# Adding each expert's rows to the output in memory with an indirect DMA, in place of one-hot products on TensorE

## Chip, cores and metric

The kernel runs on one core of one Trainium2 chip, as one launch. The metric is device time in microseconds (us), the median of several runs. TensorE is called PE here, VectorE DVE, ScalarE ACT, GpSimd POOL and SyncE SP.

## What is computed

The reference is an encoder of two layers over 256 tokens of 1024 float32 values. Layer 0 mixes with long convolutions and has a dense feed-forward part; layer 1 mixes with attention and has a mixture of 8 experts, each token going to its best two. The change touches only the mixture:

```python
def moe_swiglu(h, router, wg, wu, wd):
    ...
    logits = jnp.dot(hf, router, preferred_element_type=jnp.float32)
    top_v, top_i = lax.top_k(logits, TOP_K)
    gates = jax.nn.softmax(top_v, axis=-1).reshape(A)
    ...
    def expert_block(args):
        xe, e = args
        return (jax.nn.silu(xe @ wg[e]) * (xe @ wu[e])) @ wd[e]

    yb = lax.map(expert_block, (xb, blk_expert)).reshape(P, D)
    out = jnp.zeros((T, D), jnp.float32).at[buf_tok].add(yb.astype(jnp.float32) * buf_gate[:, None])
```

The result is `x + moe_swiglu(...)`: each expert's rows are multiplied by the gates of their tokens and added to the tokens' rows. The hidden width is 2816.

## The kernel before

**Products in parts.** Every float32 operand is split into two float32r parts, high and low (`Pair`): ACT copies the high part, DVE subtracts it from the source for the low part (`split`), and PE makes three products (`mm3`). So each half unit of weights, 128x1024, costs one ACT cast, one DVE subtraction and six products of 128x512.

**The stream of weights.** An expert's weights are 33 units of 1 MB. `weights` loads them one after another on SP's DMA queue into slots of 8 KiB per partition, and splits them by halves. Up to `N_SPLIT = 4` split halves may stand ready ahead of their products. There are 8 x 33 = 264 such loads.

**The order of the program.** The program is recorded as a plain sequence. `Plan.order` then sorts it against a simple model of the engines, gives every tile its place, and emits one queue per engine; it is the same code for the whole program. Waits are added afterwards. On the chip each engine goes through its queue in order, so an instruction that waits holds up all that stand behind it on its engine.

**An expert.** The 256 tokens stand as two tiles of 128 (`a` = 0, 1). A place of an expert is one of 128 rows that it works on. `gather` makes one-hot matrices `oh[a]` (token by place) on DVE and multiplies the tokens with them, for two experts at a time. It also transposes the one-hot matrices on PE into `ohT` (place by token). `expert` then makes six blocks of gate and up columns, each followed by the rows of down of the block before it, which sum up in two banks `py[0]`, `py[1]` (the two halves of 512 columns). At the end each bank is split into two parts, multiplied back to the tokens with `ohT`, and added to `x` with the tokens' gates:

```python
        for c in range(2):
            y = self.pair(512)
            self.split(y, py[c])
            for a in range(2):
                ps = self.bank()
                nc.tensor.matmul(ps, lhsT=ohT[:, a], rhs=y.hi, start=True, stop=False)
                nc.tensor.matmul(ps, lhsT=ohT[:, a], rhs=y.lo, start=False, stop=True)
                xa = self.x[a][:, c * 512:(c + 1) * 512]
                nc.vector.scalar_tensor_tensor(xa, ps, gate(a), xa, op0=OP.mult, op1=OP.add)
                if last:
                    self.store((a, c))
```

The last expert stores the four quarters of `x` to the output. A second round follows under `tc.If(most > 128)`, for experts with more than 128 tokens; its code is in the program, but no load of it is in the trace.

Of the kernel before, what the change touches and what calls it, by code (L numbers as in the profile page):

```python
# [21 lines left out]
D = 1024  # L22
S = 256
# [8 lines left out]
# columns of the table of per-partition scalars  # L32
# [6 lines left out]
# columns of the table of constants  # L39
K_ID, K_FLIP, K_TRI, K_ONE, K_IOTA, K_I8, K_FOLD = 0, 128, 256, 384, 512, 640, 648  # L40
N_K = 656

# [53 lines left out]
class Mem:  # L96
    """A tile: kind 'sb' (n words in the slots), 'ty' (a few words), 'ps' (a bank), 'at' (fixed)."""
# [8 lines left out]
class Slot:  # L106
    """A slot from the time it is taken until all of it is free again: of one type."""
# [22 lines left out]
LOAD = 1.3  # L130


class Plan:
# [45 lines left out]
    def pin(self, v):  # L179
        """Keep a whole slot beyond the next flush."""  # L180
        assert v.t.size == SLOT
        v.t.pinned = True
        self.fixed.append(v.t)

# [47 lines left out]
    def fits(self, op):  # L232
        """Whether the tiles that op is the first to touch can have a place now."""
# [16 lines left out]
        # what more urgent tiles will take soon  # L250
# [22 lines left out]
        if op.kind == "split" and self.n_split >= N_SPLIT:  # L273
            # only if a product waits for nothing else
            if not any(self.ops[j].n_pred == 1 and self.ops[j].eng == "tensor" for j in op.succ):
                return False
        return sum(m.kind == "ps" for m in need) <= max(0, len(self.free_bank) - banks)

# [18 lines left out]
    def cost(self, eng, fn, a, kw, aps):  # L297
        """Microseconds on the engine."""
        n = max((self.width(x) for x in aps), default=1)
        if fn == "dma_start":  # L300
            ap = aps[0]
            return self.width(ap) * ap.ap[0][1] * 4 / 360e3
# [68 lines left out]
    def order(self):  # L371
        ops = self.ops
        following = 1e9
        for op in reversed(ops):
            late = op.base
            own = op.dur + (2.0 if op.fn == "dma_start" else 0.0)
# [4 lines left out]
            if op.kind == "dense":  # L381
                # products with the stream keep their order
                op.late = following = min(op.late, following - op.dur)
# [23 lines left out]
        while done < len(ops):  # L407
            self.stuck = not events
            if self.stuck:
                # nothing runs: the most urgent operation takes from the reserves  # L410
# [20 lines left out]
            for e in engines:  # L431
                if busy[e] > t or not avail[e]:
                    continue
                if e == "sync" and dma > t + BACKLOG:
                    # loads that become urgent meanwhile go first
# [16 lines left out]
                if e in ("vector", "scalar") and op.i != self.force and op.dur > 0.2:  # L452
                    # better to wait a moment for what is more urgent
# [14 lines left out]
                else:  # L468
                    end = busy[e] = t + op.dur
                    f = op.args[2] if op.fn == "activation" else None  # L470
# [23 lines left out]
    def backwards(self):  # L494
        """Latest starts that keep to one operation at a time on every engine: the schedule from the
        end, the latest by the first estimate first."""
# [46 lines left out]
    def profile(self):  # L543
        """Slots that tiles other than the stream's hold, by the time of the latest starts."""
# [15 lines left out]
    def flush(self):  # L560
        """Order and emit what was recorded."""
        out = self.order()
        real = lambda x: x.on(self.place(x.t)) if isinstance(x, View) else x
        with self.tc.manual_schedule():
            for op in out:
                getattr(getattr(self.nc, op.eng), op.fn)(*[real(x) for x in op.args],  # L566
                                                         **{k: real(x) for k, x in op.kw.items()})
# [3 lines left out]
class Pair:  # L571
    """The two exact float32r parts of a float32 tile."""
# [16 lines left out]
def _par(t):  # L589
    """Natural order of positions -> [.., parity, place]."""  # L590
# [3 lines left out]
class _Kernel:  # L594
# [8 lines left out]
    def pair(self, n):  # L603
        """Both parts of [128, n]."""
# [45 lines left out]
    def rsqrt(self, ss, n, width):  # L650
        """(ss / width + EPS) ** -0.5, with one Newton step."""
# [10 lines left out]
    def rms(self, src):  # L662
        """One over the root mean squares of src [128, D]."""
# [8 lines left out]
    def norm_T(self, src, dst):  # L672
        """Two tiles of tokens -> the transposes of the rows over their root mean squares."""
# [15 lines left out]
    def scaled(self, dst, col, natural=False):  # L689
        """The parts of the transposes times a gain."""  # L690
# [8 lines left out]
    def head_norms(self, ps, lo, hi, rms=None):  # L699
        """Two banks of 4 heads -> the heads lo..hi-1 over their rms, two tiles."""  # L700
# [20 lines left out]
    def heads_T(self, ps, dst, scale=None, rms=None):  # L721
        """Two banks of raw heads -> dst parts [128 d, 4, 2, 128 tok]."""
# [9 lines left out]
    def dense_block(self, lhs):  # L732
        """512 columns for both token tiles: two banks."""
# [9 lines left out]
    def softmax_rows(self, ps, groups, p):  # L743
        """[128, groups, width] -> p, normalised."""
# [16 lines left out]
    def tokens(self, src):  # L761
        """[256, D] in DRAM: tile a has the tokens 2 p + a."""
# [7 lines left out]
    def rows_of(self, ps, dst, rms):  # L770
        """Two banks of rows -> parts [128, 2, 512]."""
# [3 lines left out]
    def cross(self, qps, kT, v, gain, mixT):  # L775
        """Attention over the memory."""
# [22 lines left out]
    def out_proj(self, mixT, order):  # L799
        """x += both halves of the mix by the weights of the output."""  # L800
# [23 lines left out]
    def run(self):  # L824
# [3 lines left out]
        # w_out by (q, c) within a half: the halves of a unit are (c, q)  # L828
# [19 lines left out]
        self.fold = kt[:2 * NE, K_FOLD:K_FOLD + 8]  # L848
        self.mhalf = plan.at([128, 8], "mhalf")
        nc.gpsimd.memset(self.mhalf, -0.5)  # L850
        # the sine's table, before anything waits for it
# [15 lines left out]
    def taps(self):  # L867
        """The hidden layer that makes the filters, in two versions: forward + and - backward."""
# [18 lines left out]
        # the second layer twice, for the products with both directions at once  # L887
# [7 lines left out]
        # the backward filter has no place 0  # L895
# [21 lines left out]
                # |f| + |b| is the larger of |f + b| and |f - b|  # L917
# [10 lines left out]
            # one over the sums, by channel  # L928
# [72 lines left out]
    def channels_T(self, us):  # L1001
        """Their transposes: two banks [128 tokens, 512]."""
# [92 lines left out]
    def memory(self, l, keys):  # L1095
        """Keys (transposed) or values of the memory."""
# [498 lines left out]
```

## Time and profile before

| what | value |
|---|---|
| time, median of 3 runs | 1338.82 us (1338.54 to 1339.26) |
| span of the profiled execution | 1336.3 us, 2.5 us less than the median |
| PE busy | 1316.9 us, 99% of the span |
| DVE, ACT, POOL busy | 1111.6, 918.3, 25.9 us |
| moved by DMA | 368.12 MB, 275 GB/s over the span |

The span is from the first to the last instruction of one execution; what lies around it is in the time and not in the profile. Products are pipelined: a row's duration of a product reaches from its start to its modelled end, and is longer than the distance from its start to the next one's. All recorded instructions of the plan bear line 566, where they are emitted, so groups are told apart by tiles: `s` is a slot, `b` a bank, `tiny` a few words per partition, `x` the tokens, `kt` the constants, `out` the output.

### The profile page before, as it was taken

How to read it: one execution, taken by the hardware profiler on the slowest of the kernel's cores; microseconds unless marked ns; L12 is line 12 of the kernel's file. 1: busy time of each engine (PE TensorE's matmuls, PEld its weight loads, DVE VectorE, ACT ScalarE, POOL GpSimd, SP SyncE). 2: the span in 40 equal slices, each digit the busy share in tenths (PEclk: the TensorE clock that was granted, in tenths of full speed). 3: DMA queues.
4: the chain of work that ended last, by engine and by line, in shares of the span. 5: the costliest groups of instructions: out<-in, count | busy, mean ns of one | idle time of the engine just before them, and what ended most of it. 6: DMA issues, size and time to landing. Idle time of an engine off the chain costs nothing.

```text
span 1336.3 us, 17095 instructions
## 1 busy us (share of the span) xinstructions
PE 1316.9 (99%) x6320; PEld 1087.2 (81%) x6320; DVE 1111.6 (83%) x1440; ACT 918.3 (69%) x1196; POOL 25.9 (2%) x30
## 2 busy tenths in 40 slices
PE   6999999999999999999999999999999999999997
PEld 4798888888878888888888888888888888888875
DVE  7999775554578776899999998999999999988987
ACT  7455754444566665787777777777777777777774
POOL 0100000000001000000000000000000000000000
PEclk9999999999999999999999999999999999999999
DMA  9648534357446356199899888999889898899994
GB/s 354 241 153 294 211 126 157 125 189 271 145 138 210 122 194 253 64 348 354 346 356 356 333 332 346 344 346 339 348 334 364 320 344 345 344 346 357 344 368 161
DMA packets 56430, 368.12 MB, mean 275 GB/s; under 512 B 6303, under 2 KB 10483, under 8 KB 12692
## 3 DMA queue, kind: packets, MB, share of 16 engines
q1 hardware_dynamic: 56340, 366.97, 73.9%
q8 instruction: 51, 0.84, 0.2%
q14 instruction: 39, 0.32, 0.1%
HBM read 365.87 MB, written 1.07 MB: 275 GB/s over the span
## 4 chain that ended last, share of the span: by engine, by line
PE 96%; DVE 1%; ACT 1%; issue 0%; DMA 0%; SPq 0%; DVEq 0%; ACTq 0%
PE b L566 96%; ACT s L566 1%; DVE s L566 1%; DMA sm<-sm 0%; DVE x L566 0%; SPq L566 0%; DVE tiny L566 0%; DVE cg L566 0%; DVEq L566 0%; ACTq L566 0%
## 5 line engine op out<-in xcount | busy, mean ns | idle before, releaser
L566 PE MATMUL b<-s,s 128*128 128x512 f32 (+4 forms) x5708 | 1282.3, 382 | 5.0 <-ACT s L566 4.3
L566 PEld LDWEIGHTS b<-s,s 128*128 128x128 f32 (+2 forms) x5708 | 1012.8, 188 | 213.0 <-issue 7.2
L566 DVE TENSOR_TENSOR s<-s,s 128x1024 fp32r<-128x1024 f32 (+2 forms) x729 | 839.4, 1188 | 137.4 <-ACT s L566 132.4
L566 ACT CAST s<-s 128x1024 fp32r<-128x1024 f32 (+2 forms) x705 | 710.0, 1039 | 248.1 <-PE b L566 203.9
L566 DVE TENSOR_TENSOR s<-b,s 128x512 f32<-128x512 f32 (+5 forms) x222 | 133.3, 614 | 32.2 <-ACT s L566 29.6
L566 ACT CAST s<-b 128x512 fp32r<-128x512 f32 (+3 forms) x142 | 69.8, 507 | 69.5 <-PE b L566 62.4
L566 PE MATMUL b<-kt,s 128*128 128x128 f32 (+1 forms) x496 | 88.9, 274 | 1.1 <-DVE s L566 0.9
L566 PEld LDWEIGHTS b<-kt,s 128*128 128x128 f32 x496 | 66.7, 146 | 19.4 <-ACT s L566 2.2
L566 ACT ACTIVATE s<-b 128x512 f32<-128x512 f32 (+3 forms) x81 | 42.9, 539 | 19.7 <-PE b L566 19.7
L566 DVE SCALAR_TENSOR_TENSOR s<-b,sm,s 128x256 fp32r<-128x256 f32 (+1 forms) x88 | 37.9, 477 | 8.1 <-ACT s L566 7.4
L566 ACT ACTIVATE s<-b,sm 128x256 fp32r<-128x256 f32 (+1 forms) x84 | 35.1, 484 | 12.2 <-PE b L566 7.9
L566 ACT ACTIVATE s<-b,tiny 128x256 f32<-128x256 f32 (+2 forms) x42 | 23.6, 580 | 15.4 <-PE b L566 13.5
L566 POOL TENSOR_TENSOR tiny<-tiny,mhalf 128x1 f32<-128x1 f32 (+4 forms) x23 | 25.4, 1106 | 340.8 <-DVE tiny L566 340.8
L566 PE MATMUL b<-s 128*128 128x512 f32 (+3 forms) x70 | 20.4, 380 | 5.8 <-DMA s<-fw 5.6
L566 DVE SCALAR_TENSOR_TENSOR x<-b,gate,x 128x512 f32<-128x512 f32 x32 | 22.5, 746 | 1.2 <-PE b L566 0.9
L566 ACT ACTIVATE s<-x 128x512 f32<-128x512 f32 x16 | 10.0, 630 | 14.3 <-PE b L566 5.2
L566 DVE TENSOR_TENSOR tiny<-tiny 128x1 f32<-128x1 f32 (+4 forms) x81 | 11.9, 154 | 8.3 <-ACT s L566 6.5
L566 PEld LDWEIGHTS b<-s 128*128 128x128 f32 (+1 forms) x70 | 12.2, 189 | 8.0 <-DMA s<-fw 5.6
L566 DVE TENSOR_REDUCE tiny<-b 128x2 f32<-128x512 f32 (+2 forms) x17 | 11.1, 657 | 8.3 <-PE b L566 8.3
L566 DVE TENSOR_REDUCE tiny<-s 128x4 f32<-128x512 f32 (+3 forms) x26 | 13.9, 556 | 3.6 <-ACT s L566 3.5
L566 ACT COPY s<-b 128x512 f32<-128x512 f32 x11 | 6.4, 588 | 14.6 <-PE b L566 13.8
L566 DVE TENSOR_TENSOR x<-b,x 128x512 f32<-128x512 f32 x12 | 8.2, 691 | 7.9 <-PE b L566 7.9
(57 smaller groups left out, 146.7 us busy)
## 6 DMA issues: line engine op xcount, KB each, us to landing
s<-w_moe SPq DMA_DIRECT2D x264, 1024.0 KB, 5.3
s<-w_ffn SPq DMA_DIRECT2D x33, 1024.0 KB, 5.0
s<-w_at SPq DMA_DIRECT2D x20, 1024.0 KB, 5.1
s<-w_kv SPq DMA_DIRECT2D x8, 1024.0 KB, 7.0
s<-w_hy SPq DMA_DIRECT2D x8, 1024.0 KB, 8.4
s<-w_out SPq DMA_DIRECT2D x8, 1024.0 KB, 5.0
s<-mem SPq DMA_DIRECT2D x4, 512.0 KB
x<-x SPq DMA_DIRECT2D x2, 512.0 KB
```

The costliest lines, as they stand in the source:

```text
L566: getattr(getattr(self.nc, op.eng), op.fn)(*[real(x) for x in op.args], **{k: real(x) for k, x in op.kw.items()})
```

## The change

The output tensor gets 128 more rows, which the host cuts off. At the start of the mixture `x` is stored to the output, and once more into the extra rows, so that those hold finite values. `gather` no longer makes `ohT`. A new `by_place` multiplies the one-hot matrices with four columns per token (gate high part, gate low part, row number, one) and gets for every place its gate and the number of its output row; a place without a token gets a row of its own among the extra ones. At the end of an expert each bank is scaled by the places' gates on ACT into a slot, and POOL adds the 128 rows of 2 KB to the output in memory with an indirect accumulating DMA (`add_rows`), once for each half of the columns. `self.x` is no longer updated by the experts, and the four stores at the end are gone. The planner gets two figures of its own for the new operation, `ISSUE` and `LAND`. Comments were also taken out of the file.

```diff
+ISSUE, LAND = 1.2, 4.0
...
+    def add_rows(self, out, index, rows):
+
+        self.add("gpsimd", "add_rows", (out, index, rows), {})
+
+    def emit(self, op, args, kw):
+        if op.fn == "add_rows":
+            out, index, rows = args
+            self.nc.gpsimd.indirect_dma_start(out=out, out_offset=bass.IndirectOffsetOnAxis(ap=index, axis=0), in_=rows,
+                                              in_offset=None, compute_op=OP.add)
...
+                    if op.fn == "add_rows":
+                        end += LAND
...
+        sums = plan.outside(self.out)
+        self.sums = sums.rearrange("r (c d) -> (r c) d", c=2)
+        for a in range(2):
+            nc.sync.dma_start(out=sums[:S].rearrange("(p a) d -> p a d", a=2)[:, a], in_=self.x[a])
+        nc.sync.dma_start(out=sums[S:], in_=self.x[0])
...
+            self.split(Pair(info[:, a, :, 0], info[:, a, :, 1]), g)
...
-            pt = self.bank()
-            for a in range(2):
-                self.tr(pt[:, a * 128:(a + 1) * 128], oh[a][:, i * 128:(i + 1) * 128].bitcast(F32))
-            ohT = self.slot(256, F32R)
-            nc.scalar.copy(out=ohT, in_=pt[:, :256])
-            out.append((xe[:, :, i], ohT, [t[:, i * 128:(i + 1) * 128] for t in oh]))
+            out.append((xe[:, :, i], [t[:, i * 128:(i + 1) * 128] for t in oh]))
...
+    def by_place(self, oh, info):
...
+        ps = self.bank()
+        for a in range(2):
+            nc.tensor.matmul(ps[:, :4], lhsT=oh[a], rhs=info(a), start=a == 0, stop=a == 1)
+        g, u, at = self.tiny(1), self.tiny(1), [self.tiny(1, U32) for c in range(2)]
+        nc.vector.tensor_reduce(g, ps[:, 0:2], axis=AX.X, op=OP.add)
+        nc.vector.tensor_copy(out=u, in_=ps[:, 2:3])
+        nc.vector.scalar_tensor_tensor(u, ps[:, 3:4], self.rows2[:, 3:4], u, op0=OP.mult, op1=OP.add)
+        for c in range(2):
+            nc.vector.tensor_scalar(at[c], u, self.rows2[:, 2:3], float(c), op0=OP.add, op1=OP.add)
+        return g, at
...
         for c in range(2):
-            y = self.pair(512)
-            self.split(y, py[c])
-            for a in range(2):
-                ps = self.bank()
-                nc.tensor.matmul(ps, lhsT=ohT[:, a], rhs=y.hi, start=True, stop=False)
-                nc.tensor.matmul(ps, lhsT=ohT[:, a], rhs=y.lo, start=False, stop=True)
-                xa = self.x[a][:, c * 512:(c + 1) * 512]
-                nc.vector.scalar_tensor_tensor(xa, ps, gate(a), xa, op0=OP.mult, op1=OP.add)
-                if last:
-                    self.store((a, c))
+            y = self.slot(512)
+            nc.scalar.activation(y, py[c], AF.Copy, scale=gate)
+            self.plan.add_rows(self.sums, rows[c], y)
```

Three places in the order of the program matter below. The first is PE's queue at the end of the last expert. Before, after the last products of down (into banks b4_71 and b1_68), it held the eight products with `ohT` (slot s17_7476 holds the one-hot matrix, and the other slot or the same one the parts of `y`):

```order
L566 MATMUL b4_71<-s10_10482,s17_7476 128x512 x2
L566 MATMUL b1_68<-s10_10482,s17_7476 128x512 x2
L566 MATMUL b6_73<-s17_7476 128x512
L566 MATMUL b5_72<-s17_7476 128x512
L566 MATMUL b2_69<-s10_10502,s17_7476 128x512
L566 MATMUL b4_71<-s10_10502,s17_7476 128x512
L566 MATMUL b6_73<-s17_7476 128x512
L566 MATMUL b5_72<-s17_7476 128x512
L566 MATMUL b2_69<-s10_10502,s17_7476 128x512
L566 MATMUL b4_71<-s10_10502,s17_7476 128x512
L1335 TENSOR_LOAD cnti_87
```

Now it ends with the products of down, into b3_70 (the first half of the columns) and b1_68 (the second):

```order
L298 MATMUL b3_70<-s20_10451,s19_10384 128x512 x2
L298 MATMUL b3_70<-s6_10458,s19_10384 128x512
L298 MATMUL b1_68<-s20_10451,s19_10384 128x512 x2
L298 MATMUL b1_68<-s6_10458,s19_10384 128x512
L298 MATMUL b3_70<-s6_10458,s19_10384 128x512 x2
L298 MATMUL b1_68<-s6_10458,s19_10384 128x512 x2
L1375 TENSOR_LOAD cnti_87
```

The eight last products are gone, and the last product of the first half now stands two products ahead of the end.

The second place is POOL's queue, which before held nothing in this stage. Now it holds two adds for each expert, here those of the fifth to the last (DMASW names the semaphores of POOL's own DMAs, in turn 0 to 7):

```order
L295 DMA out<-s5_8268,tiny_75 768x512 [waits DMASW7_49,DVE_49,Activation_49]
L295 DMA out<-s5_8268,tiny_75 768x512 [waits DMASW0_49,DVE_49,Activation_49]
L295 DMA out<-s9_9021,tiny_75 768x512 [waits DMASW1_49,DVE_49,Activation_49]
L295 DMA out<-s9_9021,tiny_75 768x512 [waits DMASW2_49,DVE_49,Activation_49]
L295 DMA out<-s19_9771,tiny_75 768x512 [waits DMASW3_49,DVE_49,Activation_49]
L295 DMA out<-s19_9771,tiny_75 768x512 [waits DMASW4_49,DVE_49,Activation_49]
L295 DMA out<-s20_10476,tiny_75 768x512 [waits DMASW5_49,Activation_49]
L295 DMA out<-s20_10476,tiny_75 768x512 [waits DMASW6_49,DVE_49,Activation_49]
```

Each add waits for the one ahead of it to have landed, since all of them write the same tensor.

The third place is ACT's queue at the end of the fifth expert, with the two scalings into slot s5_8268, the casts of weights behind them, and the next operation that takes the same place in that slot:

```order
L298 ACTIVATE s5_8268<-b6_73,tiny_75 128x512 [waits PE_49]
L298 ACTIVATE s5_8268<-b3_70,tiny_75 128x512 [waits PE_49]
L298 CAST s20_8278<-s8_8188 128x1024 [waits DMAHW1_49]
L298 CAST s9_8284<-s8_8188 128x1024 [waits DVE_49,PE_49]
L298 CAST s13_8295<-s16_8212 128x1024 [waits DMAHW2_49,DVE_49,PE_49]
L298 CAST s15_8301<-s16_8212 128x1024
L298 ACTIVATE s5_8268<-b4_71 128x512 [waits DMASW0_49,PE_49,Activation_49]
```

The last of these rows now waits for the first add of that expert (DMASW0), four casts behind its scaling.

## Rows read from the trace of the kernel before

**Rows 1.** The page: engines' busy time, share of the span, instructions.

```profile
PE 1316.9 (99%) x6320; PEld 1087.2 (81%) x6320; DVE 1111.6 (83%) x1440; ACT 918.3 (69%) x1196; POOL 25.9 (2%) x30
```

**Rows 2.** The page: chain that ended last, by engine.

```profile
PE 96%; DVE 1%; ACT 1%; issue 0%; DMA 0%; SPq 0%; DVEq 0%; ACTq 0%
```

**Rows 3.** Stretches: length, PE, PEld, DVE, ACT, POOL busy, granted clock, DMA share, GB/s.

```profile
540.00:562.00 22.00, 21.97 (x129) 17.96 (x129) 21.02 (x68) 16.60 (x31) 1.12 (x2) 1.00 0.01 1
640.00:940.00 300.00, 300.00 (x1379) 248.22 (x1378) 278.83 (x282) 232.25 (x265) 0.00 (x0) 1.00 0.91 344
1240.00:1326.00 86.00, 85.51 (x379) 68.11 (x378) 76.42 (x72) 63.63 (x68) 0.00 (x0) 1.00 0.84 308
```

**Rows 4.** Groups of instructions, 640 to 1240 us: busy, mean ns | idle before.

```profile
L566 DVE TENSOR_TENSOR s<-s,s 128x1024 fp32r<-128x1024 f32 x410 | 481.1, 1220 | 32.2 <-ACT s L566 29.7
L566 ACT CAST s<-s 128x1024 fp32r<-128x1024 f32 x409 | 414.0, 1052 | 89.2 <-PE b L566 72.5 <-DVE s L566 14.3 <-ACT s L566 0.8
L566 DVE TENSOR_TENSOR s<-b,s 128x512 fp32r<-128x512 f32 x45 | 30.7, 687 | 5.6 <-ACT s L566 5.1
L566 DVE SCALAR_TENSOR_TENSOR x<-b,gate,x 128x512 f32<-128x512 f32 x26 | 18.3, 746 | 1.0 <-PE b L566 0.7
```

**Rows 5.** Timeline of PE, 571 to 573 us: start, length, instructions.

```profile
571.84 0.39 PE L566 MATMUL b<-s 128*128 128x512 f32 x1
572.07 0.39 PE L566 MATMUL b<-s,s 128*128 128x512 f32 x1
572.29 0.39 PE L566 MATMUL b<-s 128*128 128x512 f32 x1
572.52 0.84 PE L566 MATMUL b<-s,s 128*128 128x512 f32 x3
```

**Rows 6.** Timeline at the start of the mixture, 536 to 582 us.

```profile
540.28 1.91 PE L566 MATMUL b<-kt,x 128*128 128x128 f32 x16
540.48 0.69 DVE L566 TENSOR_TENSOR x<-b,x 128x512 f32<-128x512 f32 x1 [0.41 <-PE b L566]
...
552.05 1.18 PE L566 MATMUL b<-mask,kt 128*128 128x8 f32 x10
...
562.36 16.11 SPq L566 DMA_DIRECT2D s<-w_moe  x6
```

**Rows 7.** The page: the costliest groups, one of DVE's small operations.

```profile
L566 DVE TENSOR_TENSOR tiny<-tiny 128x1 f32<-128x1 f32 (+4 forms) x81 | 11.9, 154 | 8.3 <-ACT s L566 6.5
```

**Rows 8.** DMA, 640 to 1240 us: packets, MB, share; loads, KB, us to landing.

```profile
q1 hardware_dynamic: 28293, 206.09, 90.6%
...
s<-w_moe SPq DMA_DIRECT2D x197, 1024.0 KB, 4.9
```

**Rows 9.** What SP's queue waited for, 640 to 1240 us: total, times, longest.

```profile
SPq L566 <- PE b L566: 349.7, 140, 6.4
SPq L566 <- DVE s L566: 172.3, 98, 4.8
```

**Rows 10.** Timeline of the end, 1326 to 1337 us.

```profile
1326.05 1.07 ACT L566 CAST s<-b 128x512 fp32r<-128x512 f32 x2 [2.58 <-PE b L566]
...
1328.17 2.73 DVE L566 SCALAR_TENSOR_TENSOR x<-b,gate,x 128x512 f32<-128x512 f32 x4 [0.22 <-PE b L566]
...
1328.96 3.20 SPq L566 DMA_DIRECT2D out<-x  x4
```

**Rows 11.** Instructions on tile `x`: ns min/median/max, first and last start; landing.

```profile
L566 SPq DMA_DIRECT2D out<-x x4: 338/580/977, 1329.0 to 1331.3; - x4
...
DMA to landing us min/median/max: 3.2/3.2/3.2
```

More of the change, by code (lines that the diff above doesn't have):

```diff
@@ L37 @@
 N_SM = 106
-K_ID, K_FLIP, K_TRI, K_ONE, K_IOTA, K_I8, K_FOLD = 0, 128, 256, 384, 512, 640, 648
-N_K = 656
+K_ID, K_FLIP, K_TRI, K_ONE, K_IOTA, K_I8, K_FOLD, K_ROW = 0, 128, 256, 384, 512, 640, 648, 656
+N_K = 660
+N_ROW = S + 128
 N_SLOT = 24
@@ L183, in pin, with outside @@
         self.fixed.append(v.t)
+    def outside(self, ap):
+        self.fixed.append(Mem("at", 0, F32, 0, ap))
+        return View(self.fixed[-1])
     def scratch(self, shape, name):
@@ L277, in fits @@
         return sum(m.kind == "ps" for m in need) <= max(0, len(self.free_bank) - banks)
+    def add_rows(self, out, index, rows):
[5 more added lines that the diff above has]
+                                              in_offset=None, compute_op=OP.add)
+        else:
+            getattr(getattr(self.nc, op.eng), op.fn)(*args, **kw)
     @staticmethod
@@ L299, in cost @@
         n = max((self.width(x) for x in aps), default=1)
+        if fn == "add_rows":
+            return ISSUE
         if fn == "dma_start":
@@ L375, in order @@
             late = op.base
-            own = op.dur + (2.0 if op.fn == "dma_start" else 0.0)
+            own = op.dur + (2.0 if op.fn == "dma_start" else LAND if op.fn == "add_rows" else 0.0)
             for j in op.succ:
@@ L565, in flush @@
             for op in out:
-                getattr(getattr(self.nc, op.eng), op.fn)(*[real(x) for x in op.args],
-                                                         **{k: real(x) for k, x in op.kw.items()})
+                self.emit(op, [real(x) for x in op.args], {k: real(x) for k, x in op.kw.items()})
         self.reset()
@@ L848, in run @@
         self.fold = kt[:2 * NE, K_FOLD:K_FOLD + 8]
+        self.rows2 = kt[:, K_ROW:K_ROW + 4]
         self.mhalf = plan.at([128, 8], "mhalf")
@@ L1272, in moe_layer @@
         cnti = plan.at([128, 1], "cnti", I32)
+        meta = plan.at([128, 8 * NE], "meta", F32R)
+        info = meta.rearrange("p (a e j) -> p a e j", a=2, j=4)
+        nc.vector.tensor_scalar(info[:, :, :, 3], self.ones[:, :2 * NE].rearrange("p (a e) -> p a e", a=2), 1.0, None,
+                                op0=OP.mult)
+        for a in range(2):
+            nc.vector.tensor_scalar(info[:, a, :, 2], self.ones[:, :NE], self.rows2[:, a:a + 1], None, op0=OP.mult)
+        sums = plan.outside(self.out)
[3 more added lines that the diff above has]
+        nc.sync.dma_start(out=sums[S:], in_=self.x[0])
         pick = lambda t, a: t[:, a * NE:(a + 1) * NE]
@@ L1330, in moe_layer @@
             for j, xo in enumerate(self.gather([col(place, e), col(place, e + 1)])):
-                self.expert(xo, col(gate, e + j), e + j == NE - 1, None if e + j else first)
+                self.expert(xo, lambda a, e=e + j: info[:, a, e], None if e + j else first)
         plan.flush()
@@ L1338, in moe_layer @@
             nc.vector.memset(cur, 0.0)
+            own = plan.at([128, 8], "own", F32R).rearrange("p (a j) -> p a j", a=2)
             nc.vector.tensor_scalar(place, place, -128.0, None, op0=OP.add)
@@ L1350, in moe_layer @@
                         nc.vector.tensor_reduce(cl[:, 2 * i + a:2 * i + a + 1], d, axis=AX.X, op=OP.add)
+                for a in range(2):
+                    nc.vector.tensor_scalar(own[:, a, 2:], info[:, a, 0, 2:].bitcast(F32), 1.0, None, op0=OP.mult)
+                    self.split(Pair(own[:, a, 0:1], own[:, a, 1:2]), cl[:, 2 + a:3 + a])
                 self.w = self.weights([io["w_moe"][ds(e, 1), i].rearrange("z p n -> (z p) n") for i in range(NUNIT)])
                 xo, = self.gather([lambda a: cl[:, a:a + 1]])
-                self.expert(xo, lambda a: cl[:, 2 + a:3 + a], False)
+                self.expert(xo, lambda a: own[:, a])
                 plan.flush()
-            self.store()
-            plan.flush()
     def gather(self, places):
@@ L1379, in gather, with expert @@
         for i in range(len(places)):
-            pt = self.bank()
-            for a in range(2):
-                self.tr(pt[:, a * 128:(a + 1) * 128], oh[a][:, i * 128:(i + 1) * 128].bitcast(F32))
-            ohT = self.slot(256, F32R)
-            nc.scalar.copy(out=ohT, in_=pt[:, :256])
-            out.append((xe[:, :, i], ohT, [t[:, i * 128:(i + 1) * 128] for t in oh]))
-        return out
-    def store(self, only=None):
-        ov = self.out.rearrange("(p a) d -> p a d", a=2)
+            out.append((xe[:, :, i], [t[:, i * 128:(i + 1) * 128] for t in oh]))
+        return out
+    def by_place(self, oh, info):
+        nc = self.nc
+        ps = self.bank()
         for a in range(2):
-            for c in range(2):
-                if only in (None, (a, c)):
-                    at = slice(c * 512, (c + 1) * 512)
-                    self.nc.sync.dma_start(out=ov[:, a, at], in_=self.x[a][:, at])
-    def expert(self, xo, gate, last, first=None):
+            nc.tensor.matmul(ps[:, :4], lhsT=oh[a], rhs=info(a), start=a == 0, stop=a == 1)
[6 more added lines that the diff above has]
+        return g, at
+    def expert(self, xo, info, first=None):
         nc = self.nc
-        xe = xo[0]
-        ohT = xo[1].rearrange("p (a t) -> p a t", a=2)
+        xe, oh = xo
+        gate, rows = self.by_place(oh, info)
         def block():
@@ L1417, in act @@
                 for i, (a, t) in enumerate((a, t) for a in range(2) for t in (first[a].hi, first[a].lo)):
-                    nc.tensor.matmul(g, lhsT=xo[2][a], rhs=t, start=i == 0, stop=i == 3)
+                    nc.tensor.matmul(g, lhsT=oh[a], rhs=t, start=i == 0, stop=i == 3)
                 nc.scalar.copy(out=sg, in_=g)
@@ L1477, in _constants @@
     k[:, K_FOLD:K_FOLD + 8] = np.tile(np.eye(8), (16, 1))
+    for i in range(2):
+        k[:, K_ROW + i] = 2 * (2 * np.arange(128) + i)
+    k[:, K_ROW + 2] = 2 * (S + np.arange(128))
+    k[:, K_ROW + 3] = -k[:, K_ROW + 2]
     c["consts"] = k
@@ L1590 @@
     aps = {k: nc.dram_tensor(k, list(a.shape), F32, kind="ExternalInput").ap() for k, a in io.items()}
-    out = nc.dram_tensor("out", [S, D], F32, kind="ExternalOutput").ap()
+    out = nc.dram_tensor("out", [N_ROW, D], F32, kind="ExternalOutput").ap()
     build(nc, aps, out)
     r = bass_utils.run_bass_kernel_spmd(nc, [io], core_ids=[0])
-    return np.asarray(r.results[0]["out"]).reshape(1, S, D)
+    return np.asarray(r.results[0]["out"])[:S].reshape(1, S, D)
```

## The prediction

> **What bounds the kernel now.** I read the page first. PE is busy for 99% of the span [rows 1], and the chain that ended last lies on PE for 96% [rows 2]. A busy PE need not be PE at its peak, so I went to the stage of the experts. In 300 us of it PE had no gap at all and the granted clock was 1.00, the upper of its two levels, 2.4 GHz [rows 3]. Single products start 0.227 us apart: three of them between 571.84 and 572.52 us [rows 5]. So in this stage a product that is taken out of PE's queue gives back 0.227 us, as long as nothing behind PE is just as full.
>
> Two things stand close behind. DVE is busy for 278.83 of 300 us, 93%, and the 16 DMA engines for 91% [rows 3]. The groups show what kind of nearness that is: ACT's casts stood idle 89.2 us in 600, of which 72.5 us for PE, and DVE's subtractions mostly waited for ACT [rows 4]. Both work to PE's measure. SP's queue, which issues the loads, waited 349.7 us for PE and 172.3 us for DVE out of 600 us [rows 9]; it waits for slots to come free, not for the DMA engines. 409 casts in 600 us are 1.467 us for a half unit, and 66 halves make 96.8 us for an expert [rows 4]. PE sets this pace.
>
> **What goes from PE.** An expert loses eight products of 128x512. For seven experts these stand inside the stage: 56 x 0.227 = 12.7 us. Those of the last expert stand behind its last product of down and belong to the end, below. Sixteen transposes for `ohT` go too; sixteen of the same shape took 1.91 us [rows 6], so 1.9 us.
>
> **What comes to PE.** `by_place` has two products of four columns per expert, 16 in all. The trace does not have them. The nearest row is ten products of eight columns in 1.18 us, 0.12 us each [rows 6]; that makes 1.9 us at most. The lower end is nothing. Those in the row are whole float32 and the new ones float32r with half the columns, so I take the middle, 1.0 us. PE gains 12.7 + 1.9 - 1.0 = 13.6 us, between 12.7 and 14.6.
>
> **DVE and ACT.** Per expert DVE loses two subtractions of 0.687 us and four additions to `x` of 0.746 us [rows 4], 4.4 us, and gets five operations on one column at about 0.154 us [rows 7], 0.8 us. From 93% of 96.8 us, 90.0 us, it comes to 86.4 us. PE's new pace is 96.8 - 13.6 / 7 = 94.9 us, so DVE will be at 91%, no fuller than now. ACT loses two casts and a copy and gets two scalings of the same size; I count it as nothing, since ACT is busy for 232.25 of 300 us [rows 3].
>
> **The stores of `x` at the start of the mixture.** Three DMAs of 512 KB are put into SP's queue, ahead of loads. `x` is complete at 541.2 us (540.48 + 0.69), and the next load is issued at 562.36 us [rows 6]; from 540 to 562 us the DMA engines moved 1 GB/s [rows 3]. At 344 GB/s the 1.6 MB take 4.6 us of that hole. I count nothing. Without the hole the loads behind would be 4.6 us later.
>
> **The end.** Before, ACT starts on the last sums at 1326.05 us [rows 10] and the span ends at 1336.3 us: 10.25 us for split, products, additions, four stores and the closing. The last store is issued at 1331.3 us and lands 3.2 us later [rows 11], so 1.8 us are left for closing. Now the first half is complete two products (0.45 us) before the last one, and a scaling takes about 0.6 us, as a cast of that shape [rows 10]; the first add can go 0.15 us after the last product. The second add waits for the first to land. With x from one add's start to its landing, the end takes 0.15 + 2x + 1.8 us.
>
> The trace has no such DMA, so x is bounded. Not below 3.2 us, the plain store of the same 256 KB [rows 11]; not above that store plus a whole load of four times the size, 3.2 + 4.9 = 8.1 us [rows 8, 11], since an add has to read its target before it writes. I take 5.0 us, nearer to the store, because the bytes are the store's; the planner's own figures in the diff make 5.2. The end then takes 11.95 us, 1.7 us more than before (from 1.9 less to 7.9 more).
>
> The Trainium skill, "DMA: Bandwidth & Descriptors", section "Anatomy of one DMA — SWDGE (gpsimd) path", gives a fit for a DMA issued from POOL of about 2.0 us plus the bytes over 436 GB/s. That is an estimate of 2.6 us for 256 KB without the time to write the descriptors, and with it the end would take 3.1 us less than before and the kernel 1322.1 us. No run here shows it yet.
>
> **Sum.** The span of 1336.3 us loses 13.6 and gains 1.7: 1324.4 us. The span is 2.5 us below the median of the runs; with these the time is **1326.9 us**. Its own range is from 1336.3 - 14.6 - 1.9 + 2.5 = 1322.3 to 1336.3 - 12.7 + 7.9 + 2.5 = 1334.0 us.
>
> **Rival 1: the adds come late, and the kernel is slower.** Every slot and every small tile that an add reads is freed only when it has landed. The tightest place is the fifth expert: ACT's next use of the slot stands four casts behind the scaling, 4 x 1.467 = 5.9 us. I counted the others in the queues: the second expert leaves 5.9 us too, on DVE, the third and fourth 7.3 us, and the sixth 11.7 us for both of its adds. PE has up to four split halves in hand, another 5.9 us, so a stall reaches it only beyond that. At x = 5.0 none of these waits. At x = 10 the end costs 11.7 us more than before, and the sixth expert stalls PE by 20 - 11.7 - 5.9 = 2.4 us: that eats the 13.6 us. From there on the kernel is slower; at x = 12 the end costs 15.7 us more, and the sixth expert 6.4, the first 3.4 (its room is ten casts, 14.7 us): 1338.8 - 13.6 + 25.5 = 1351 us. For it speaks that the adds run beside a DMA load of 91%; against it that a 1 MB load lands in 4.9 us under the same load [rows 8]. Chance 0.10.
>
> **Rival 2: the stream of loads becomes the bound.** 206.09 MB in 600 us at 90.6% [rows 8] are 379 GB/s with all engines busy. An expert's 34.6 MB would then take 91.3 us, and PE's new pace is 94.9 us: 3.6 us are spare. An expert's adds are 0.52 MB. If the engines carry them three times (source, target, back) that is 4.1 us, 0.5 us too much: some 4 us in all, 1331 us. If rows of 2 KB cost the engines twice as much, it is 4.6 us an expert and the gain is gone, less what was loaded ahead: I put that at 1340 us. SP's waits for PE and DVE speak against it [rows 9]. Chance 0.16, of which half with a gain, three parts in eight without a difference, one slower.
>
> **Rival 3: POOL and DVE hold each other up.** DVE spends 481.1 of 600 us in subtractions of 1.22 us that read two slots [rows 4], and POOL has to read its list of rows between them. If an add is kept waiting for two of these, x is 7.5 us in the stream. The room of 5.9 us is missed by 1.6 us twice, that of 7.3 by 0.2 us twice and that of 11.7 by 3.3 us. The split halves in hand cover it; if they are gone, it costs 6.9 us, 1334 us. No row before shows POOL issuing a DMA beside DVE. The Trainium skill, "SBUF — State Buffer", section "SBUF: two separate sides", says that an operation of DVE with two SBUF inputs holds back an instruction of POOL that reads SBUF, and that a POOL DMA grew from 620 to 3100 ns beside DVE; that rule speaks against the change. Chance 0.08.
>
> **Rival 4: the time taken from PE is not used,** because the conversions already run at its pace and another order of the queues loses as much: 1338.8 us. PE's gapless stretch and ACT's waits for PE speak against it [rows 3, 4]. Chance 0.04.
>
> **How the numbers follow.** The forecast has 0.62. About 0.2%, 2.7 us, is what a measurement of this kernel can tell from no change. Faster: 0.62, rival 3 and half of rival 2, 0.78. Same: rival 4 and 0.06 of rival 2, 0.10. Slower: rival 1 and 0.02, 0.12. From 1322 us, the lower end of the forecast, to 1337 us lie the forecast, rival 3 and the better half of rival 2: 0.78, which is the range.
>
> **What the profile will show.** If I am right: 56 products fewer between the first and the last expert, PE still without gaps at 0.227 us a product, an expert in about 95 us, DVE at about 91%; the last product some 13.6 us earlier, near 1312.5 us; POOL's adds landing some 5 us after their start, and about 12 us from the last product to the end of the span. Wrong in size: the landing of an add, seen twice at the end. Wrong in kind: casts or subtractions that wait for an add of POOL, PE's loads of weights waiting for ACT or DVE behind them, or a first cast of a unit that waits for its load.

## The result, and the profile after

The changed kernel takes **1359.8 us** (median of 4 runs, 1357.4 to 1363.8), beside 1338.7 us of the kernel before on the same chip. The ratio is 1.016, 95% interval 1.0147 to 1.0171: slower, where faster was predicted. The profiled execution took 1361.4 us, with a span of 1359.7 us.

The page, as in [rows 1, 2], with the group of the adds (busy time, mean ns; idle time before and its main releaser):

```profile
PE 1318.6 (97%) x6256; PEld 1079.9 (79%) x6256; DVE 1086.6 (80%) x1437; ACT 918.1 (68%) x1190; POOL 54.5 (4%) x46
...
PE 41%; DMA 4%; DVE 2%; ACT 2%; issue 1%; POOL 0%; POOLq 0%; ACTq 0%; DVEq 0%
...
L295 POOL DMA_INDIRECT out<-s,tiny x16 | 27.7, 1731 | 780.3 <-ACT s L298 375.2
```

PE has 64 instructions fewer and is busy longer. The chain that ended last, 96% PE before, can now be followed back for only half the span, and there DMA stands in it. These are its adds (start, length to the landing):

```profile
849.29 10.23 DMA out<-s,tiny
...
948.77 9.55 DMA out<-s,tiny
...
1041.39 9.57 DMA out<-s,tiny
...
1146.12 12.11 DMA out<-s,tiny
...
1159.01 6.68 DMA out<-s,tiny
...
1348.24 4.54 DMA out<-s,tiny
```

Five of the six lie beside the loads of weights and take 6.7 to 12.1 us; the sixth, at the end with nothing beside it, takes 4.5 us. Over all sixteen adds, the view of the tile `out` gives this landing (least, median, most):

```profile
DMA to landing us min/median/max: 4.5/8.1/12.1
```

The prediction worked with 5.0 us everywhere. Without the two adds at the end, the fourteen in the stream took 5.1 to 12.1 us, with a median of 8.5. Who waited, 560 to 1360 us (total, times, longest):

```profile
PEld b L298 <- DVE s L298: 20.2, 33, 3.2
ACT s L298 <- DMA out<-s,tiny: 15.9, 3, 6.5
PEld b L298 <- ACT s L298: 11.5, 3, 6.3
DVE tiny L298 <- DMA out<-s,tiny: 10.7, 4, 3.6
PE b L298 <- ACT s L298: 10.2, 3, 5.9
PE b L298 <- DVE s L298: 6.4, 7, 2.7
```

ACT waited for slots that an add was still reading, DVE for small tiles. PE and its loads of weights (PEld) then waited for ACT and DVE; most of the 33 waits in the first row are short and not due to adds, as e1_own and e6_own_rate show below. The timeline shows the first of these stalls, at the end of the first expert (start, length, instructions, idle time before):

```profile
654.24 1.25 ACT L298 ACTIVATE s<-b,tiny 128x512 f32<-128x512 f32 x2
...
655.21 2.51 POOL L295 DMA_INDIRECT out<-s,tiny  x1 [108.14 <-DVE tiny L298]
...
667.18 1.54 POOL L295 DMA_INDIRECT out<-s,tiny  x1 [9.46 <-DVE s L298]
...
668.32 1.05 ACT L298 CAST s<-s 128x1024 fp32r<-128x1024 f32 x1 [0.91 <-PE b L298]
...
668.47 4.58 PE L298 MATMUL b<-s,s 128*128 128x512 f32 x19
...
675.89 0.59 ACT L298 CAST s<-b 128x512 fp32r<-128x512 f32 x1 [6.52 <-DMA out<-s,tiny]
...
678.92 5.27 PE L298 MATMUL b<-s,s 128*128 128x512 f32 x13 [5.87 <-ACT s L298]
```

The second add starts 12.0 us after the first. (The row names DVE as its releaser; DVE had long been done, and the instruction waits for the first add as well.) ACT is ready for the slot at 669.4 us and gets it at 675.9. PE works on for 3.7 us out of what was split ahead, to 673.05, and starts 3.0 us after ACT does. So 6.5 us of waiting on ACT become 5.9 on PE.

The stretches show what follows a stall (columns as in [rows 3]):

```profile
660.00:680.00 20.00, 14.13 (x63) 11.38 (x62) 11.40 (x11) 10.41 (x13) 1.54 (x1) 0.91 0.82 305
...
676.00:684.00 8.00, 5.08 (x13) 4.03 (x14) 5.92 (x7) 6.74 (x8) 0.00 (x0) 0.57 0.31 112
1040.00:1060.00 20.00, 16.45 (x59) 12.34 (x58) 11.27 (x11) 10.77 (x12) 3.09 (x2) 0.83 0.92 308
1160.00:1180.00 20.00, 17.38 (x60) 13.03 (x61) 13.57 (x15) 11.31 (x13) 0.55 (x1) 0.83 0.76 259
```

In each the granted clock falls, to 0.57 in the eight microseconds from 676 us on: most of these at the lower level, 1.2 GHz. Thirteen products in 5.08 busy us are 0.39 us each, beside 0.227 [rows 5].

The end, which answers to [rows 10]:

```profile
1343.66 4.03 PE L298 MATMUL b<-s,s 128*128 128x512 f32 x17
...
1347.28 1.27 ACT L298 ACTIVATE s<-b,tiny 128x512 f32<-128x512 f32 x2 [2.76 <-PE b L298]
1348.24 1.54 POOL L295 DMA_INDIRECT out<-s,tiny  x1 [85.62 <-ACT s L298]
1353.56 1.54 POOL L295 DMA_INDIRECT out<-s,tiny  x1 [3.78 <-DMA out<-s,tiny]
```

From ACT's start on the last sums to the end of the span are 12.4 us, where 11.95 were predicted. The second add starts 5.32 us after the first, and 6.1 us after that the span ends.

### The profile page after: what moved, and what is told of

The parts are those of the page before. It is cut to its first block, busy times and chain, and to the rows that moved or that the text cites. A ratio compares the mean times of both kernels' runs of the same rounds, so it can differ in the third digit from the quotient of the medians.

```text
span 1359.7 us, 17037 instructions
## 1 busy us (share of the span) xinstructions
PE 1318.6 (97%) x6256; PEld 1079.9 (79%) x6256; DVE 1086.6 (80%) x1437; ACT 918.1 (68%) x1190; POOL 54.5 (4%) x46
## 4 chain that ended last, share of the span: by engine, by line
PE 41%; DMA 4%; DVE 2%; ACT 2%; issue 1%; POOL 0%; POOLq 0%; ACTq 0%; DVEq 0%
PE b L298 41%; DMA out<-s,tiny 4%; DVE s L298 2%; ACT s L298 2%; POOL out L295 0%; DVE tiny L298 0%; POOLq L1375 0%; ACTq L298 0%; DVEq L298 0%; POOLq L295 0%
## 5 line engine op out<-in xcount | busy, mean ns | idle before, releaser
L298 PE MATMUL b<-s,s 128*128 128x512 f32 (+2 forms) x5676 | 1291.4, 385 | 21.3 <-ACT s L298 13.8
L298 PEld LDWEIGHTS b<-s,s 128*128 128x128 f32 (+1 forms) x5676 | 1010.6, 189 | 238.6 <-DVE s L298 20.7
L298 ACT CAST s<-s 128x1024 fp32r<-128x1024 f32 (+1 forms) x705 | 711.6, 1039 | 257.0 <-PE b L298 206.8
L298 DVE TENSOR_TENSOR s<-b,s 128x512 f32<-128x512 f32 (+5 forms) x206 | 122.6, 607 | 35.7 <-ACT s L298 30.4
L298 ACT CAST s<-b 128x512 fp32r<-128x512 f32 (+3 forms) x118 | 58.3, 504 | 67.8 <-PE b L298 54.6
L295 POOL DMA_INDIRECT out<-s,tiny x16 | 27.7, 1731 | 780.3 <-ACT s L298 375.2
L298 ACT ACTIVATE s<-b,tiny 128x512 f32<-128x512 f32 (+2 forms) x58 | 34.0, 612 | 21.2 <-PE b L298 19.6
L298 DVE TENSOR_TENSOR tiny<-tiny 128x1 f32<-128x1 f32 (+4 forms) x81 | 12.1, 155 | 10.1 <-ACT s L298 8.1
L298 DVE TENSOR_REDUCE tiny<-b 128x2 f32<-128x512 f32 (+3 forms) x25 | 12.3, 494 | 9.7 <-PE b L298 9.7
L298 DVE TENSOR_TENSOR s<-b,tiny 128x512 f32<-128x512 f32 (+3 forms) x26 | 13.8, 558 | 0.1
L298 ACT ACTIVATE s<-s,tiny 128x256 f32<-128x256 f32 (+1 forms) x24 | 13.0, 579 | 0.7 <-DVE tiny L298 0.6
```

Of the source, the lines that this page charges most:

```text
L295: self.nc.gpsimd.indirect_dma_start(out=out, out_offset=bass.IndirectOffsetOnAxis(ap=index, axis=0), in_=rows, in_offset=None, compute_op= ...
L298: getattr(getattr(self.nc, op.eng), op.fn)(*args, **kw)
```

## The experiments

Two theories stood against each other. **W**: adds that land late make ACT and DVE wait, PE behind them, and the clock drops after each stall. **D**: the adds' traffic makes the stream of loads the bound. A third loss was suspected, in the order that the planner makes. Ratios are to the kernel before on the same chip.

**e1_own: the same adds, but nothing near waits for them.** The scaled results go into quarters of `self.x`, which no expert reads once it has been split and stored, and the row numbers into a tile of their own. (A name `n` for the expert is handed down.)

```diff
+        self.places = plan.at([128, 2 * NE], "places", U32)
...
-        g, u, at = self.tiny(1), self.tiny(1), [self.tiny(1, U32) for c in range(2)]
+        g, u, at = self.tiny(1), self.tiny(1), [self.places[:, 2 * n + c:2 * n + c + 1] for c in range(2)]
...
-            y = self.slot(512)
+            y = self.x[n % 2][:, c * 512:(c + 1) * 512]
```

> The scaled results lie in quarters of the token tile that is free by then, and the row numbers in a tile of their own, so that nothing but the scaling of the expert after next waits for an add. The adds themselves stay. Theory W (the time went into waits behind late adds and into the lower clock after each): no gap of TensorE above 1 us, granted clock 1.00 from the first expert to the last, and 1338.8 - 13.6 (products taken out) + 2 (end) + 7 (order of transposes) = about 1334 us, 1328 to 1337. Theory D (the adds' traffic makes the stream of loads the bound): 1350 us or more, with first casts that wait for loads.

Measured: 1335.7 us (1334.7 to 1337.2), ratio 0.998 (0.9966 to 0.9987). PE has no gap above 0.7 us from 560 us to its last product, and the granted clock is 1.00. The adds land no sooner than in the changed kernel:

```profile
DMA to landing us min/median/max: 4.6/9.9/11.1
```

So 24.1 us of the changed kernel's time are waits behind adds and what follows them. Theory D falls: the same adds run in the same stream. Time, gaps and clock are as theory W expected.

**e2_land: only the planner's figures.**

```diff
-ISSUE, LAND = 1.2, 4.0
+ISSUE, LAND = 1.5, 12.0
```

> Only the two figures by which the planner orders the queues change: issue 1.5 us, landing 12.0 us of an add (were 1.2 and 4.0). Every wait for an add stays. Theory W: the planner puts its readers late enough, and the time is that of the variant with tiles of its own, 1334 +- 4 us. Theory D: 1350 us or more, as with own tiles. If only a part of the waits can be moved, in between, with stalls left at places that the planner cannot move.

Measured: 1336.2 us (1335.2 to 1336.8), ratio 0.9975 (0.9965 to 0.9985). The adds still read slots and small tiles, and they still land late:

```profile
DMA to landing us min/median/max: 4.4/8.8/11.2
```

But no row is left in which ACT or DVE waits for an add, and PE has no gap above 0.7 us. Two figures bring back 23.6 us. The stalls came from an order made for adds of 5.2 us, in which the readers stand too close behind.

**e4_lastonly: without the traffic.** The adds of seven experts are left out (their results are missing from the output).

```diff
+            if n == NE - 1:
-            self.plan.add_rows(self.sums, rows[c], y)
+                self.plan.add_rows(self.sums, rows[c], y)
```

> As the variant with tiles of its own, with the adds of the last expert alone (those of seven experts are left out). Theory W: within 2 us of the variant with all adds, since nothing waits for them there and they cost the stream nothing. Theory D: 10 us or more below it.

Measured: 1336.5 us (1334.2 to 1337.1), within 1 us of e1_own. The adds cost the stream nothing that can be measured.

**Why an add lands late: e3_plain, p1_loads, p2_dve.** e3_plain is e1_own without `compute_op`. p1_loads and p2_dve put work that nobody needs beside the two adds at the end: eight loads of 1 MB, or fourteen subtractions of 128x1024 with two inputs.

The first is the edit of p1_loads, the second that of p2_dve:

```diff
+            if n == NE - 1 and c == 0:
+                for i in range(8):
+                    t = self.slot()
+                    nc.scalar.activation(t[:, :1], py[0][:, :1], AF.Copy, scale=gate)
+                    nc.sync.dma_start(out=t, in_=self.io["w_moe"][0, i])
```

```diff
+            if n == NE - 1 and c == 0:
+                for i in range(14):
+                    t = self.slot(1024)
+                    nc.vector.tensor_tensor(out=t.rearrange("p (i n) -> p i n", i=2), in0=y.unsqueeze(1).to_broadcast([128, 2, 512]), in1=y.unsqueeze(1).to_broadcast([128, 2, 512]), op=OP.subtract)
```

> As the variant with tiles of its own, but the indirect DMA writes its rows and adds nothing (the sum over experts is left out). If the landing of 8 to 12 us in the stream is the price of accumulating (reading the target, adding), it falls to about 5 us here, and the two at the end to about 3 us. If it is waiting behind loads, it stays at 7 to 12 us in the stream. The time is within 3 us of the variant that accumulates by theory W, and 5 us or more below it by theory D (a third of the bytes).

> The variant with tiles of its own, and beside the adds of the last expert eight loads of 1 MB that nobody reads (the two adds at the end landed 4.5 us after their start with nothing beside them). If loads in the DMA engines' queues are what keeps an add from landing, these two adds now land after 8 to 12 us. If it is DVE's use of memory, they stay at 4.5 us. The time of the kernel says nothing here.

> The variant with tiles of its own, and beside the adds of the last expert fourteen subtractions of 128x1024 on DVE that nobody needs, with two inputs in SBUF each, and no loads. If DVE holds back POOL (the rule of the Trainium skill, 'SBUF — State Buffer', section 'SBUF: two separate sides'), these two adds take 1 to 2 us more to issue and land after 6 us or more. If loads are the cause, issue stays at about 1.5 us and landing at 4.5 us.

Measured, in one execution each: the two adds at the end on POOL's timeline, where the second waits for the first to land. First e1_own, then p1_loads, p2_dve and e3_plain:

```profile
1321.46 1.54 POOL L295 DMA_INDIRECT out<-x,places  x1 [84.43 <-ACT x L298]
1326.89 1.54 POOL L295 DMA_INDIRECT out<-x,places  x1 [3.89 <-DMA out<-x,places]
```

```profile
1323.28 1.54 POOL L295 DMA_INDIRECT out<-x,places  x1 [85.01 <-ACT x L298]
1335.45 1.54 POOL L295 DMA_INDIRECT out<-x,places  x1 [10.63 <-DMA out<-x,places]
```

```profile
1326.13 2.40 POOL L295 DMA_INDIRECT out<-x,places  x1 [90.43 <-ACT x L298]
1332.36 1.84 POOL L295 DMA_INDIRECT out<-x,places  x1 [3.83 <-DVE s L298]
```

```profile
1322.28 0.96 POOL L295 DMA_INDIRECT out<-x,places  x1 [86.24 <-ACT x L298]
1325.77 0.96 POOL L295 DMA_INDIRECT out<-x,places  x1 [2.54 <-DMA out<-x,places]
```

(The row of p2_dve names DVE as its releaser; the first add had landed 0.8 us before, as in the other runs.) In p1_loads PE and DVE stood idle beside the two adds, and the DMA engines were busy all the time (columns as in [rows 3]):

```profile
1323.00:1345.00 22.00, 0.00 (x0) 0.00 (x0) 0.00 (x0) 0.58 (x2) 3.09 (x2) 0.56 1.01 365
```

From start to start are 5.4 us alone, 12.2 beside loads, 6.2 beside DVE, and 3.5 for a write that adds nothing. Loads are the cause of the late landing: they add 6.7 us. DVE comes out between its two expected cases: it lengthens the issue on POOL by 0.3 to 0.9 us, and the distance from start to start by 0.8. Accumulating costs 1.9 us alone; among the loads the plain writes land in 7.5 us (median), the adds of e1_own in 9.9. The view of `out` in e3_plain, with the undisturbed landing as the least:

```profile
DMA to landing us min/median/max: 2.7/7.5/9.4
```

The one run of e3_plain took 1331.8 us, 3.9 less than e1_own, where theory W allowed 3. The whole difference lies at the end: from the first add's start to the end of the span are 7.7 us in e3_plain and 11.6 in e1_own. The last product stands no earlier (1321.3 and 1320.5 us), so the stream is not faster without the accumulating.

**Slots or small tiles: e9_y_only.** The results in `self.x` as in e1_own, the row numbers in the small tiles as in the changed kernel.

> As the changed kernel, but the scaled results alone lie in the token tile; the row numbers stay in the small tiles that rotate. Of the waits in the changed kernel, 15.9 us in three were ACT's for slots and 10.7 us in four DVE's for small tiles. If each kind stalls TensorE by itself, the stalls behind small tiles stay (TensorE's gaps near 858 and 1158 us, 7 us with the lower clock after them another 6): 1342 to 1350 us. If the slots alone are to blame, it comes down to the 1335.7 us of the variant with both.

Measured: 1349.0 us (1346.3 to 1352.7), ratio 1.008 (1.0064 to 1.009). Its waits and a stretch:

```profile
DVE tiny L298 <- DMA out<-x,tiny: 10.3, 3, 5.0
```

```profile
1140.00:1160.00 20.00, 15.71 (x64) 12.29 (x63) 12.44 (x16) 9.75 (x12) 2.60 (x1) 0.91 0.81 280
```

One column of 512 bytes is enough: DVE waits for a small tile, and PE and its clock follow. Of the 24.1 us, 10.8 go with the slots and 13.3 with the small tiles, taken away in this order; the other order (row numbers alone in a tile of their own) was not run.

**The order: e6_own_rate, e8_before_rate, e10_after_rate.** One figure of the planner changes, what it takes a load to last, in e1_own, in the kernel before and in the changed kernel:

```diff
-            return self.width(ap) * ap.ap[0][1] * 4 / 360e3
+            return self.width(ap) * ap.ap[0][1] * 4 / 385e3
```

> As the variant with tiles of its own, and the planner reckons loads at 385 GB/s instead of 360. If the time of a stream of 64 products is lost by the place where the planner puts the transposes (it thinks that the loads bind), this gives 3 to 7 us: 1329 to 1333 us. If the loads do bind there, it gives nothing or loses.

> The kernel before, with the planner's loads at 385 GB/s and nothing else changed. If the figure of 360 costs the changed kernel more because the change makes TensorE's demand come closer to it, this gains little here: 0 to 3 us, 1336 to 1339. If the figure costs every version the same, it gains 8 us, 1331, and then none of the 8 us belongs to the change.

> The changed kernel with all its waits, and the planner's loads at 385 GB/s. If waits and order are two losses that add, it gains the 8 us that the variant with tiles of its own gained: 1352 us, 1346 to 1356, with stalls of TensorE as before. If another order happens to move readers away from the adds, 1330 to 1340.

| kernel | us (runs) | ratio to before |
|---|---|---|
| e6_own_rate | 1327.5 (1323.6 to 1327.8) | 0.9905 (0.989 to 0.9919) |
| e8_before_rate | 1335.4 (1334.1 to 1335.9) | 0.997 (0.996 to 0.9983) |
| e10_after_rate | 1354.1 (1348.1 to 1355.9) | 1.010 (1.0082 to 1.0117) |

The figure is worth 8.2 us in e1_own and 3.6 us in the kernel before, so some 4.6 us of it belong to the change. Both gains are above their expected ranges (3 to 7 us, and 0 to 3 if the figure costs the change more), and the 5.7 us of e10_after_rate are fewer than the 8 expected. In stretches of e1_own PE starts 13 or 14 products fewer in 100 us than in e6_own_rate, with the clock at 1.00 in both:

```profile
1040.00:1140.00 100.00, 99.16 (x455) 80.19 (x454) 89.38 (x94) 77.05 (x88) 4.98 (x3) 1.00 0.97 358
1140.00:1240.00 100.00, 99.43 (x440) 78.68 (x439) 88.64 (x89) 77.61 (x83) 5.91 (x3) 1.00 0.98 366
```

```profile
1040.00:1140.00 100.00, 100.00 (x468) 83.10 (x467) 91.65 (x98) 80.13 (x93) 4.42 (x3) 1.00 1.00 382
1140.00:1240.00 100.00, 100.00 (x454) 82.67 (x453) 90.64 (x90) 79.14 (x87) 5.84 (x3) 1.00 0.96 371
```

The last column says why the figure was wrong: the loads come at up to 382 GB/s when they are asked for. With the slower stretches go small waits. In e1_own, PE's loads of weights waited for DVE's subtractions, 560 to 1340 us:

```profile
PEld b L298 <- DVE s L298: 13.1, 29, 0.7
```

In e6_own_rate:

```profile
PEld b L298 <- DVE s L298: 0.4, 1, 0.4
```

That the planner took the loads for the bound is argued from its own figures: at 360 GB/s, 33 loads last 96.1 us, between PE's 96.8 us for an expert before and the 94.9 predicted after. In e10_after_rate starts of products lie 1.3 to 5.8 us apart at seven places, so this figure alone doesn't move the readers away from the adds.

**One add for an expert: e5_one, e7_one_rate.** 128 rows of 4 KB in place of twice 128 of 2 KB (the row numbers then count whole rows; those lines are left out here); e5_one is otherwise e1_own, e7_one_rate is e6_own_rate.

```diff
+        y = self.x[n % 2]
...
-            y = self.slot(512)
-            nc.scalar.activation(y, py[c], AF.Copy, scale=gate)
-            self.plan.add_rows(self.sums, rows[c], y)
+            nc.scalar.activation(y[:, c * 512:(c + 1) * 512], py[c], AF.Copy, scale=gate)
+        self.plan.add_rows(self.sums, rows[0], y)
```

> As the variant with tiles of its own, but one add an expert, 128 rows of 4 KB, in place of two of 128 rows of 2 KB. The end then holds one landing instead of two: some 3 us shorter, since 512 KB land later than 256 KB (5 to 6 us instead of 4.5), so 1331 to 1334 us. If the fixed part of an add is small, the end is no shorter, and the time that of the variant with two adds.

> Tiles of its own, one add an expert, and the planner's loads at 385 GB/s. The gains of the two parts lie at different places (the end: 2.9 us; the order of the queues: 8.2 us), so they should add: 1335.7 - 2.9 - 8.2 = 1324.6 us, 1322 to 1328.

Measured: e5_one 1332.8 us (1332.3 to 1334.3), 2.9 less than e1_own; e7_one_rate **1321.7 us** (1321.7 to 1322.0), ratio 0.987 (0.9855 to 0.9884). That beats both kernels, and lies 0.3 us below the expected range. It is 5.8 us below e6_own_rate, not 2.9: in the profile of e6_own_rate the clock dropped once in the first layer (0.83 from 60 to 70 us), and at the second expert it is 2.5 us behind e7_one_rate (649.5 and 647.0 us). Why the clock dropped there stays open; without it the 8.2 us above would be some 2.5 more, if the other runs of e6_own_rate had the drop too.

How far each had come (us; first cast of an expert's first load, and the last product, which before and in e8_before_rate is one with `ohT`):

| | before | changed | e1_own | e7_one_rate | e8_before_rate |
|---|---|---|---|---|---|
| 2nd expert | 645.9 | 643.1 | 644.3 | 647.0 | 646.3 |
| 4th | 837.6 | 841.5 | 834.6 | 836.2 | 838.5 |
| 6th | 1030.4 | 1036.8 | 1024.6 | 1025.6 | 1031.3 |
| 8th | 1226.6 | 1248.4 | 1221.7 | 1213.1 | 1225.4 |
| last product | 1328.4 | 1347.3 | 1320.5 | 1310.7 | 1325.7 |

ACT's start on the last sums, in e8_before_rate and in e7_one_rate:

```profile
1322.83 0.59 ACT L566 CAST s<-b 128x512 fp32r<-128x512 f32 x1 [3.51 <-PE b L566]
```

```profile
1310.46 1.37 ACT L298 ACTIVATE x<-b,tiny 128x512 f32<-128x512 f32 x2 [3.54 <-PE b L298]
```

## Why the prediction was wrong

- **The step that failed** is the sentence "At x = 5.0 none of these waits". For x, the time from an add's start to its landing, the bounds were 3.2 to 8.1 us, and one value, 5.0, was used for the end and for the stream. At the end it held: 4.5 us. In the stream the landing was 5.1 to 12.1 us, in the median 8.5, and two adds in a row took 20.6 us (from 655.2 us to the landing at 675.8) where 10 were reckoned with. So ACT and DVE waited for adds, PE behind them, and that took the 24.1 us. The 5.0 leaned on the planner's 5.2, the very figure that e2_land shows to be wrong here. The upper bound was built from a load of 1 MB that lands in 4.9 us [rows 8]. But that is a load in its own queue; p1_loads shows what an add from POOL takes beside queued loads, 12.2 us from start to start instead of 5.4.
- **The rooms** in rival 1 were counted rightly: at the first expert ACT wanted the slot at 669.4 us, 15 us after the first scaling began, where 14.7 were counted. **The reserve of PE** was not 5.9 us. It was 3.7 us, and PE started 3.0 us after ACT did: a wait of ACT reached PE nearly whole.
- **The clock** was in no term. Between e1_own and the changed kernel the last products lie 26.8 us apart. Nine gaps of PE make 18.4 us (distances between starts above 0.7 us, less 0.227 each). The other 8.4 us are what is left. They fit the stretches at the lower clock (in e1_own the granted clock is 1.00 from 560 us on); no run separates them.
- **Rival 1**, at 0.10, was the right mechanism with a price that comes near by luck: 1351 us at x = 12. Of its 25.5 us, 15.7 stood at the end, where x was 4.5 and only some 2 us were lost; stalls had 9.8, at the first and the sixth expert, and cost 24, for want of clock and reserve. PE's gaps lie at the first and at the third to the sixth. e9_y_only puts over half of the loss behind the small tiles.
- **PE's gain** of 13.6 us was about right. With the planner's figure mended in both, ACT starts on the last sums at 1322.8 us in e8_before_rate and at 1310.5 us in e7_one_rate: 12.4 us, and 13.0 counted from the second expert on. With the figure as it was, only 5.5 us came out: the last product of e1_own stands at 1320.5 us, and before, ACT started on the last sums at 1326.05 [rows 10]. **DVE** is at 91% from 1040 to 1240 us in e6_own_rate, as predicted. **The stores of `x`** cost nothing that can be seen: the second expert begins earlier in the changed kernel than before, and PE has no gap where they run.
- **The end** came out at 12.4 us for 11.95, in part by luck. x was 4.5 for 5.0, but the first add started 0.96 us after ACT where 0.15 were reckoned, and the second 0.8 us after the first had landed where nothing was: 0.96 + 5.32 + 6.1 us for 0.15 + 5.0 + 6.8.
- **The order** was argued away in rival 4. It cost 8.2 us, of which the kernel before had 3.6 as well. This is the second step that failed: with every wait for an add gone, e1_own is only 3.3 us faster than the kernel before, where 11.9 were forecast.
- **Rival 2** falls by e4_lastonly. **Rival 3** is small: 0.8 us in p2_dve. The rule of the Trainium skill, "SBUF — State Buffer", section "SBUF: two separate sides", has the right sign here (the issue of an add took 2.40 and 1.84 us beside DVE for 1.54), but the fivefold growth that it tells of shows in no run (3.50 us at most).

The predicted 1326.9 us is about the time of e6_own_rate, 1327.5 us: what the change gives once no reader waits for an add and the order fits. That the two agree is in part chance, for the kernel before gains 3.6 us from the same figure. Beside it, at 1335.4 us, the change is worth 7.9 us, and not the 11.9 that were forecast.

## What to carry to other kernels

An operation that is new to a kernel should be timed beside the traffic it will meet; its time alone is a lower bound. Where a planner or a scheduler orders queues by a figure, the figure is part of the change: here two numbers were worth 24 us, and a third one 8. Everything that a slow DMA reads, down to an index column, stays taken until it has landed; give these tiles places of their own before you count on a reserve elsewhere.

## What the runs showed of the hardware

- An indirect DMA of 256 KB that accumulates landed in 4.6 us alone, a plain one in 2.7; among the loads 9.9 and 7.5 (medians of e1_own and e3_plain over all sixteen). The fit in the Trainium skill, "DMA: Bandwidth & Descriptors", section "Anatomy of one DMA — SWDGE (gpsimd) path", makes an estimate of 2.6 us: the plain write alone agrees, and it holds for neither an add nor a queue beside it.
- One add of 512 KB landed in 6.2 us alone (e7_one_rate; 6.9 in e5_one), two of 256 KB one after the other took 10 us. So one larger add was cheaper here.
- POOL took 0.96 us to issue the plain write and 1.54 for the add, up to 3.50 in the stream (e1_own).
- After PE's longest stall, 5.9 us, the granted clock was at its lower level, 1.2 GHz, for most of eight microseconds (0.57). The nine gaps, 18.4 us, went with another 8.4 us, so stalls cost about half as much again: an estimate from the difference to e1_own.
